# The first two modulation chunks in quarters, and the queries of layer 1 behind their keys

## The chip, the cores and the metric

The kernel runs on one core of a Trainium2 chip. The metric is device time of one launch in microseconds, the median of the runs. TensorE (PE) multiplies matrices, VectorE (DVE) and ScalarE (ACT) work on tiles elementwise, GpSimd (POOL) does a few elementwise jobs, and SyncE (SP) issues nearly all loads. Each engine works through its own list of instructions in order; semaphores tie the lists together.

## The reference

The program is a transformer of two layers on 256 tokens x and 256 context tokens, width 1024, all in float32. In a layer, nine modulation chunks of 1024 numbers are computed from the conditioning vectors and a weight `w_ada`. The first two of layer 0 are the shift and the scale of its first feed-forward block:

```python
silu_c = jax.nn.silu(c)
silu_cc = jax.nn.silu(c_ctx)
for l in range(DEPTH):
    mx = jnp.split((silu_c @ w_ada[l] + b_ada[l])[:, None, :], N_MOD, axis=-1)
    mc = jnp.split((silu_cc @ w_ada[l] + b_ada[l])[None, None, :], N_MOD, axis=-1)
    x = x + 0.5 * mx[2] * swiglu(modulate(rms_norm(x, norm_g[l, 0]), mx[0], mx[1]), w_ffn1_gu[l], w_ffn1_down[l])
    # the same for h_ctx with mc
    zx = modulate(rms_norm(x, norm_g[l, 1]), mx[3], mx[4]) @ w_in[l]
    zc = modulate(rms_norm(h_ctx, norm_g[l, 1]), mc[3], mc[4]) @ w_in[l]
    # split zx, zc: neighbourhood attention (qa, ka, va), window attention with rotary
    # positions (qb, kb, vb), convolution (u), three gates; merged, added to x; then a second ffn
```

`modulate(h, shift, scale)` is `h * (1 + scale) + shift`, and `swiglu` is `(silu(a) * b) @ w_down` with a and b the halves of `h @ w_gu`.

## The kernel before

**Tiles.** Activations lie with features on the 128 partitions: the residual is eight tiles `R[k]` of 128 x 512, x in the left half of the columns and context in the right. A weight block is 128 x 128. All float32 products are made of three faster ones: a number is split into a high part h (written by ACT, line 123) and the rest l (written by DVE, line 124), and `mm3` (lines 317 to 319) adds h·h, h·l and l·h. The weight stream `W` loads eight blocks at a time (`raw`, 512 KB, line 274, four buffers) and splits four at a time into `wh` and `wl`. A pool of 62 slots of 128 x 516 holds the other tiles.

**The start.** Class `FirstNorm` begins the first feed-forward block. With A = g(1 + scale) from chunk 1 and B = shift from chunk 0, the block's input is H = A·R·rs + B, where rs is one number per token from the sum of squares. To have work before rs is known, the first four output columns of the gate-and-up weight are multiplied with Q = A·R (`scale`, lines 511 and 512), and rs is applied to the result. These four results are the PSUM tiles `f` (12 `mm3` steps a feature tile, 96 matmuls for all eight). What B adds to them is a separate small product (`fb`, `fc`). Chunk 1 therefore stands ahead of all, and chunk 0 is needed only for H.

A chunk comes in two halves of four feature tiles. `ada_load` (line 190) loads a half as eight `araw` tiles of 256 KB. `ada_first` multiplies them with silu(c) (line 200; 32 output rows a matmul, four column groups), DVE copies the result (`adas`, 207), PE transposes it (`adat`, 209), and DVE adds the bias into `mod` (212) and, for chunk 1, makes `modA` (176, 178). `blocks` writes the whole start out in the order in which every engine is to do it, and `in_order` ties it so: half 0 of chunk 1, Q of tiles 0 to 3, all four columns on these, squares, half 1, Q of tiles 4 to 7, the columns on these, rs (`inv_rms`, lines 338 to 360), then `nt` = A·R·rs (459), chunk 0, `fb` (598), and Hh and Hl (484, 485). From `g` on, PE streams over the remaining 40 columns.

**Layer 1's attention.** `middle` runs over 12 attention steps: three head pairs of the neighbourhood attention, then three of the window attention, two query halves each. A step makes scores (`sc`, line 1008), a softmax (`pf`, 1041 to 1053), transposes (`pt`, 1069) and the product with the values (`pv`, 1088). Between these, PE is filled from a list of parts: gates, the window attention's keys (`key_b`), its queries (`query_b`), and merges. A key or query of the window attention passes through `rope`: ACT scales it (896), DVE makes four products with the sine (899), POOL multiplies and adds (901, 902), and ACT and DVE split it into `kbh` or `qx`. The order of the parts is a written list; `step` takes from it at an even rate, and more where a query is due.

Of the kernel before, what the change touches and what calls it, by code (L numbers as in the profile page):

```python
# [23 lines left out]
DFF = 2816  # L24
KF = 22
GRID_W = 64
# [35 lines left out]
WB, WS = 8, 4  # L62
# [25 lines left out]
def dit_block_kernel(ctx, tc, xT, vec, ident_d, const, crow, gfin, rpb, ws, ada0, adaT, out):  # L88
# [17 lines left out]
    def S(dt=F32, name="s"):  # L106
        return slots.tile([P, 2 * NQ], dt, tag="s", name=nm(name))
# [8 lines left out]
    def PS(name="ps"):  # L116
        return psum.tile([P, NT], F32, tag="ps", name=nm(name))
# [66 lines left out]
                out=modG[l][:, br], in0=src, scalar1=0.5, scalar2=None, op0=ALU.mult  # L184
            )

    def ada_load(ch, h):
        raws = [S(name="araw") for _ in range(KD)]
        for k in range(KD):
            nc.sync.dma_start(raws[k][:, :NT], ada0[ch, h, k])  # L190
        return raws

    def ada_first(ch, raws):

        for h in range(2):
            pa = PS("ada")
            for k in range(KD):
                raw = raws[h][k]
                for j in range(4):
                    nc.tensor.matmul(  # L200
                        pa[32 * j:32 * j + 32, :P], cs[:, k, :], raw[:, j * P:(j + 1) * P],
                        start=(k == 0), stop=(k == KD - 1),
                    )
                if k < KD - 1:
                    yield
            sa = S(name="adas")
            nc.vector.tensor_copy(sa[:, :P], pa[:, :P])
            pt = PS("adat")
            nc.tensor.transpose(pt[:, :P], sa[:, :P], ident)
            ks = slice(4 * h, 4 * h + 4)  # L210
            o = V_BADA + ch * KD
            nc.vector.tensor_tensor(
                out=mod[0][:, ch * KD + ks.start:ch * KD + ks.stop, :],
                in0=pt[:, :P].rearrange("p (j q) -> p j q", q=32)[:, :, 0:2],
                in1=vt[:, o + ks.start:o + ks.stop].unsqueeze(2).to_broadcast([P, 4, 2]), op=ALU.add,
            )
            mod_chunk(0, ch, ks)
            yield

    class Ada:  # L220

# [41 lines left out]
    class Stream:  # L263
# [38 lines left out]

        def col(self, name, l, c, n=KD):
            return [self.one(name, l, k * P, c) for k in range(n)]

        def wide(self, name, l, r, cs):
            o = (self.pos % WS) * P
# [195 lines left out]
    class FirstNorm(Norm):  # L503
# [19 lines left out]
            in_order(self.begin, self.end, N_AFTER)  # L523

        def blocks(self, fns):
            wts, pss, gens, res = [], [], [], []

            def block():
                wts.append(fns[len(wts)]())
                pss.append(PS("f"))  # L530
                gens.append(steps(pss[-1], wts[-1], self.Q, slice(0, NT)))

            def go(gen, n=1):
                for _ in range(n):
                    next(gen, None)

            def load_x(ks):
                for k in ks:
                    nc.sync.dma_start(R[k], xT[:, k, :])


            raws = [ada_load(1, 0)]
            W.load()
            load_x(range(4))
            W.load()
            load_x(range(4, KD))
            W.load()
            W.load()
            raws.append(ada_load(1, 1))
            chunk = ada_first(1, raws)  # L550
            go(chunk, KD)
            zero = [ada_load(0, 0), ada_load(0, 1)]
            W.load()
            zero = ada_first(0, zero)
            self.scale(0)
            block()
            go(gens[0])
            for k in range(1, 4):
                self.scale(k)
                go(gens[0])  # L560
            block()
            go(gens[1], 4)
            for k in range(4):
                self.square(k, nc.vector)
            block()
            go(gens[2], 4)
            for k in range(4, KD):
                self.square(k, nc.vector)
            block()
            go(gens[3], 4)  # L570
            norm = inv_rms([self.sq], self.nq, oneD, res)
            go(chunk, KD)
            for k in range(4, KD):
                self.scale(k)
                go(gens[0])
            go(norm)
            go(gens[1], 4)
            go(norm)
            self.rs = res[0]
            go(gens[2], 4)  # L580
            nts = [self.normed(k) for k in range(KD - N_POOL)]
            go(zero, KD)
            go(gens[3], 4)


            b = mod[0][:, :KD, :]
            bb = cpool.tile([P, KD, 4], F32R, name="bb")
            n = len(wts)
            self.H, brs = [], []
            for h in range(2):  # L590
                ks = slice(4 * h, 4 * h + 4)
                split(bb[:, ks, 0:2], bb[:, ks, 2:4], b[:, ks])
                self.hidden(range(4 * h, min(4 * h + 4, KD - N_POOL)), nts)
                pb = PS("fb")
                for i, w in enumerate(wts):
                    for k in range(ks.start, ks.stop):
                        for j in range(2):
                            nc.tensor.matmul(
                                pb[:4, i * P:(i + 1) * P], bb[:, k, :], w[k][j],
                                start=k == ks.start and j == 0, stop=k == ks.stop - 1 and j == 1)  # L600
                br = S(name="br")
                nc.vector.tensor_copy(br[:4, :n * P], pb[:4, :n * P])
                brs.append(br)
                if h == 0:
                    go(zero, KD)
            for _ in range(N_EARLY):
                W.make()
            self.end = traced()
# [34 lines left out]
    def ffn(l, br, norm, nxt, ada_end=None):  # L643
# [7 lines left out]
        pend = norm.first([lambda c=c: W.col(name + "_gu", l, c) for c in cols[:nf]], 3)  # L651
        if ada_end:
            ada.enter(mod[l][:, 3 * br * KD, 0:1])
        n0 = ada.n
# [43 lines left out]
    def middle(l, norm, nxt):  # L698
# [563 lines left out]
def pack(inputs, plan):  # L1262
# [33 lines left out]
            blk = a[name][l, r:r + P, c:c + P]  # L1296
        ws[i // WB, :, i % WB] = blk

    ada0 = np.ascontiguousarray(a["w_ada"][0][:, :2 * D].reshape(KD, P, 2, 2, NT).transpose(2, 3, 0, 1, 4))
# [8 lines left out]

SHAPES = {
    "xT": (P, KD, NT), "vec": (P, V_N), "ident_d": (P, P), "const": (P, C_N), "crow": (2, D), "gfin": (1, D),  # L1310
    "rpb": (DEPTH, 6, P, 6 * GRID_W), "ws": (N_WT // WB, P, WB * P), "ada0": (2, 2, KD, P, NT), "adaT": (N_ADA, P, D),
}


# [16 lines left out]
```

## Time and profile before

| | |
|---|---|
| median of 3 runs | 1968.12 us (1966.95 to 1969.37) |
| profiled execution | 1965.63 us, span 1963.8 us |
| PE busy | 1938.2 us (99%) |
| DVE, ACT, POOL busy | 71%, 46%, 5% |
| PE's longest idle times after the first 60 us | 2.80 us and 1.51 us, both in layer 1's attention |
| granted clock, mean | 0.997 |

A row of the timeline gives start and duration in us, engine, line, operation, tiles out<-in, shapes and count; in brackets stands the idle time of the engine ahead of it and what ended that. Rows of the same kind that follow each other are merged, so the duration of a row with x8 covers eight instructions. A row of the windows gives, for each engine, busy us and instructions in a stretch, then the clock granted to PE, the DMA engines' busy share and the rate in GB/s. The profiled execution was 2.5 us below the median of the runs.

### The profile page before, as it was taken

Reading aid. Unit: us, or ns where it says so; the run is one execution under the profiler, and the core shown is the slowest. Engines: PE = TensorE matmul, PEld = TensorE weight load, DVE = VectorE, ACT = ScalarE, POOL = GpSimd, SP = SyncE. Lnnn points to the kernel's source line nnn. Section 1 sums busy time; section 2 is a strip of 40 time slices with the busy share of each in tenths; the row PEclk is TensorE's granted clock in tenths of the full one; section 3 lists DMA queues with packets and bytes.
Section 4 is the critical chain, followed back from the end, with each engine's and each line's share of the span. In section 5 each row is a group of like instructions: output and inputs, shape, how many; then the busy total and the mean of one; then the engine's idle time right before and its main releaser. Section 6 shows DMA issues by size and latency. Waiting matters only on the chain. (4 is left out here: it accounts for less than half of the span.)

```text
span 1963.8 us, 29316 instructions
## 1 busy us (share of the span) xinstructions
PE 1938.2 (99%) x10748; PEld 1649.4 (84%) x10748; DVE 1401.6 (71%) x3190; ACT 896.9 (46%) x1765; POOL 104.4 (5%) x100
## 2 busy tenths in 40 slices
PE   7999999999999999999999999999999999999998
PEld 4788888897888888988888888888888988999998
DVE  5897667779777546976667569666675897887654
ACT  3533232353767634533323344332223567866553
POOL 0000000100011101000000110000001001120000
PEclk9999999999999999999999999999999999999999
DMA  8365454522221222354444435544544243355553
GB/s 306 129 237 171 161 182 161 183 89 95 85 71 65 97 95 89 120 180 150 160 162 161 159 110 174 168 144 159 164 157 142 95 146 117 129 183 182 184 185 106
DMA packets 82655, 287.39 MB, mean 146 GB/s; under 512 B 9296, under 2 KB 11088, under 8 KB 82128
## 3 DMA queue, kind: packets, MB, share of 16 engines
q1 hardware_dynamic: 79488, 277.91, 42.9%
q0 software_dynamic: 864, 4.98, 0.7%
q10 hardware_dynamic: 2160, 2.64, 0.5%
q8 instruction: 84, 1.38, 0.3%
q14 instruction: 59, 0.48, 0.1%
HBM read 284.44 MB, written 1.05 MB: 145 GB/s over the span
## 5 line engine op out<-in xcount | busy, mean ns | idle before, releaser
L123 ACT ACTIVATE wh<-raw 128x512 fp32r<-128x512 f32 x760 | 463.9, 627 | 541.0 <-PE g L318 163.4
L124 DVE TENSOR_TENSOR wl<-raw,wh 128x512 fp32r<-128x512 f32 x760 | 520.4, 695 | 161.6 <-ACT wh L123 156.5
L244 DVE CUSTOM_DVE_ANT_0 junk<-araw,phase 128x512 f32<-128x512 f32 x512 | 353.3, 690 | 231.0 <-DMA araw<-in_adaT_dram 220.8
L319 PE MATMUL g<-Hh,wl 128*128 128x512 f32 (+1 forms) x1240 | 455.2, 367 | 0.0
L318 PE MATMUL g<-Hl,wh 128*128 128x512 f32 (+1 forms) x1240 | 454.4, 366 | 0.0
L317 PE MATMUL g<-Hh,wh 128*128 128x512 f32 (+1 forms) x1240 | 454.3, 366 | 0.0
L317 PEld LDWEIGHTS g<-Hh,wh 128*128 128x128 f32 x1240 | 233.3, 188 | 41.4 <-ACT wh L123 0.3
L318 PEld LDWEIGHTS g<-Hl,wh 128*128 128x128 f32 x1240 | 233.0, 188 | 41.4
L319 PEld LDWEIGHTS g<-Hh,wl 128*128 128x128 f32 x1240 | 232.9, 188 | 40.8
L317 PE MATMUL pr<-gh,wh 128*128 128x512 f32 (+1 forms) x704 | 257.7, 366 | 0.0
L319 PE MATMUL pr<-gh,wl 128*128 128x512 f32 (+1 forms) x704 | 257.5, 366 | 0.0
L318 PE MATMUL pr<-gl,wh 128*128 128x512 f32 (+1 forms) x704 | 257.0, 365 | 0.0
L317 PE MATMUL b<-Hh,wh 128*128 128x512 f32 (+1 forms) x480 | 166.1, 346 | 0.0
L318 PE MATMUL b<-Hl,wh 128*128 128x512 f32 (+1 forms) x480 | 163.1, 340 | 0.0
L319 PE MATMUL b<-Hh,wl 128*128 128x512 f32 (+1 forms) x480 | 163.0, 340 | 0.0
L123 ACT ACTIVATE gh<-g 128x512 fp32r<-128x512 f32 (+1 forms) x88 | 50.7, 576 | 234.2 <-DVE g L685 226.6
L318 PEld LDWEIGHTS pr<-gl,wh 128*128 128x128 f32 x704 | 132.4, 188 | 23.2
L319 PEld LDWEIGHTS pr<-gh,wl 128*128 128x128 f32 x704 | 132.4, 188 | 23.0
L317 PEld LDWEIGHTS pr<-gh,wh 128*128 128x128 f32 x704 | 132.2, 188 | 22.9
L317 PE MATMUL f<-qh,wh 128*128 128x258 f32 (+1 forms) x408 | 123.0, 302 | 4.0 <-ACT wh L123 2.4
L319 PE MATMUL f<-qh,wl 128*128 128x258 f32 (+1 forms) x408 | 120.2, 295 | 1.1 <-DVE wl L124 1.1
L318 PE MATMUL f<-ql,wh 128*128 128x258 f32 (+1 forms) x408 | 120.5, 295 | 0.0
(246 smaller groups left out, 2590.1 us busy)
## 6 DMA issues: line engine op xcount, KB each, us to landing
raw<-in_ws_dram SPq DMA_DIRECT2D x380, 512.0 KB, 3.6
araw<-in_adaT_dram SPq DMA_DIRECT2D x128, 512.0 KB, 4.2
araw<-in_ada_dram SPq DMA_DIRECT2D x32, 256.0 KB, 5.4
phase<-in_crow_dram POOLq DMA_DIRECT2D x3, 1024.0 KB, 5.8
tb<-in_rpb_dram ACTq DMA_DIRECT2D x12, 192.0 KB, 2.6
R<-in_xT_dram SPq DMA_DIRECT2D x8, 256.0 KB, 6.3
phase<-in_const_dram POOLq DMA_DIRECT2D x2, 640.0 KB, 6.6
out_dram<-fin SPq DMA_DIRECT2D x4, 256.0 KB, 2.5
```

What stands on the lines that cost most here:

```text
L123: nc.scalar.activation(out=hi, in_=src, func=AF.Copy)
L124: nc.vector.tensor_tensor(out=lo, in0=src, in1=f32(hi), op=ALU.subtract)
L244: nc.vector.tensor_tensor_reduce(out=junk, in0=raw[:, c], in1=self.rows[:, s, c], scale=1.0, scalar=0.0, op0=ALU.mult, op1=ALU.add, accum_ ...
L317: nc.tensor.matmul(ps, wh, xh, start=start, stop=False)
L318: nc.tensor.matmul(ps, wh, xl, start=False, stop=False)
L319: nc.tensor.matmul(ps, wl, xh, start=False, stop=stop)
```

## The change

It has two parts.

**The start.** A chunk is loaded and computed by quarters of two feature tiles. A quarter has four `araw` tiles of 256 KB (the bytes of a chunk stay the same); each holds rows of two feature blocks, so that the sums over the even and the odd ones land in different column groups, and the transpose becomes a product with `sel`, a 128 x 4 matrix that adds the two. The 16 rows of weights that the four columns need are taken by feature tile, not by column: the list `ws` is packed in the order of use, so one `wh` now holds one feature tile of all four columns. Loads are queued quarter by quarter: four `araw`, one `raw`, two `R`; chunk 0 comes behind all of them. The work goes by feature tile: weights, Q, the four columns' products, and so on, with the next quarter's chain between.

```diff
+    sel = cpool.tile([P, 4], F32, name="sel")
     def ada_first(ch, q, raws):
+        for i, raw in enumerate(raws):
+            for h in range(2):
+                for j in range(2):
+                    o = 2 * h + j
                     nc.tensor.matmul(
+                        pa[32 * o:32 * o + 32, :P], cs[:, 2 * i + h, :], raw[:, o * P:(o + 1) * P],
+                        start=(i == 0), stop=(i == len(raws) - 1),
+        nc.vector.tensor_copy(sa[:, :P], pa[:, :P])
+        yield
+        nc.tensor.matmul(pt[:, :4], sa[:, :P], sel, start=True, stop=True)
 ...
+            a = ada_first(1, 0, raws[0])
+            go(a)
+            go(a)
+            for q in range(4):
+                k = 2 * q
+                if q < 2:
+                    raws.append(ada_load(1, q + 2))
+                    W.load()
+                    load_x(k + 4, k + 5)
+                weights(k)
+                self.scale(k)
+                prod(k)
+                if q < 3:
+                    a = ada_first(1, q + 1, raws[q + 1])
+                    go(a)
+                weights(k + 1)
+                self.scale(k + 1)
+                if q == 3:
+                    break
+                prod(k + 1, range(2))
+                go(a)
+                prod(k + 1, range(2, n))
+                self.square(k, nc.vector)
+                self.square(k + 1, nc.vector)
+            zero = [ada_load(0, q) for q in range(4)]
+            W.load()
+            W.load()
+            self.square(KD - 2, nc.vector)
+            self.square(KD - 1, nc.vector)
             norm = inv_rms([self.sq], self.nq, oneD, res)
+            prod(KD - 1, [0, 1])
+            z = [ada_first(0, q, raws) for q, raws in enumerate(zero)]
 ...
```

Behind this stand chunk 0's four quarters with the rest of tile 7's products, rs, `fb`, `nt` and H between them.

On DVE, the order before, from the end of a half's chain (`mod`, `modA`): the Q of four tiles and the weights of two columns follow at once.

```order
L212 TENSOR_TENSOR mod_103<-adat_192,vt 128x8
L176 TENSOR_SCALAR modt_195<-mod_103 128x8
L178 TENSOR_TENSOR modA_104<-modt_195,vt 128x8
L512 SCALAR_TENSOR_TENSOR ql_233<-R_79,modA_104,qh_232 128x256 x2
L124 TENSOR_TENSOR wl_239<-raw_125,wh_238 128x512
L124 TENSOR_TENSOR wl_243<-raw_125,wh_242 128x512
L512 SCALAR_TENSOR_TENSOR ql_251<-R_80,modA_104,qh_250 128x256 x2
L512 SCALAR_TENSOR_TENSOR ql_260<-R_81,modA_104,qh_259 128x256 x2
L512 SCALAR_TENSOR_TENSOR ql_269<-R_82,modA_104,qh_268 128x256 x2
```

Now, from the end of one quarter's chain to the end of the next:

```order
L178 TENSOR_TENSOR modA_104<-modt_322,vt 128x4
L396 TENSOR_TENSOR sq_245<-sq_245,sq_331 128x512
L396 TENSOR_TENSOR sq_245<-sq_245,sq_334 128x512
L124 TENSOR_TENSOR wl_338<-raw_172,wh_337 128x512
L522 SCALAR_TENSOR_TENSOR ql_342<-R_83,modA_104,qh_341 128x256 x2
L213 COPY adas_376<-ada_359 128x128
L124 TENSOR_TENSOR wl_379<-raw_172,wh_378 128x512
L522 SCALAR_TENSOR_TENSOR ql_383<-R_84,modA_104,qh_382 128x256 x2
L219 TENSOR_TENSOR mod_103<-adat_394,vt 128x4
L176 TENSOR_SCALAR modt_397<-mod_103 128x4
L178 TENSOR_TENSOR modA_104<-modt_397,vt 128x4
```

The squares' additions moved ahead of the next tile's weights and Q, and the copy of a quarter's result (`adas`) stands behind the first tile's Q.

On PE, at the same place, before: the two halves of a column's work enclose one chain.

```order
L319 MATMUL f_350<-qh_268,wl_343 128x512
L200 MATMUL ada_363<-araw_141,cs_100 32x128 x4
L200 MATMUL ada_363<-araw_142,cs_100 32x128 x4
L200 MATMUL ada_363<-araw_143,cs_100 32x128 x4
L200 MATMUL ada_363<-araw_144,cs_100 32x128 x4
L200 MATMUL ada_363<-araw_145,cs_100 32x128 x4
L200 MATMUL ada_363<-araw_146,cs_100 32x128 x4
L200 MATMUL ada_363<-araw_147,cs_100 32x128 x4
L200 MATMUL ada_363<-araw_148,cs_100 32x128 x4
L209 MATMUL adat_398<-ident,adas_396 128x128
L317 MATMUL f_246<-qh_404,wh_242 128x512
```

Now (the last of a tile's twelve products, the next quarter's chain, and half of the next tile's products ahead of `adat`):

```order
L329 MATMUL f_114<-qh_341,wl_338 128x512
L208 MATMUL ada_359<-araw_250,cs_100 32x128 x4
L208 MATMUL ada_359<-araw_251,cs_100 32x128 x4
L208 MATMUL ada_359<-araw_252,cs_100 32x128 x4
L208 MATMUL ada_359<-araw_253,cs_100 32x128 x4
L327 MATMUL f_111<-qh_382,wh_378 128x512
L328 MATMUL f_111<-ql_383,wh_378 128x512
L329 MATMUL f_111<-qh_382,wl_379 128x512
L327 MATMUL f_112<-qh_382,wh_378 128x512
L328 MATMUL f_112<-ql_383,wh_378 128x512
L329 MATMUL f_112<-qh_382,wl_379 128x512
L216 MATMUL adat_394<-sel,adas_376 128x4
```

The chain is entered four times instead of two, each time behind twelve products, and its second half behind six more.

**Layer 1's list of parts.** The number of parts is the same; the window attention's keys and first query come after six gates, the other queries after two more.

```diff
-            parts = [query(2), *some(0, 8), *some(2, 1), key_b(), query_b(0), *some(2, 3), query_b(1),
-                     *some(2, 4), query_b(2), *some(1, 4)]
+            parts = [query(2), *some(0, 6), key_b(), query_b(0), *some(0, 2), query_b(1), query_b(2),
+                     *some(2, 8), *some(1, 4)]
```

On ACT, before, ahead of the first scores of the window attention (`qx_14828` is their query; the keys were split a step earlier):

```order
L1053 ACTIVATE pf_13979<-pf_13979,st_14795 128x512
L1053 ACTIVATE pf_13980<-pf_13980,st_14801 128x512
L896 ACTIVATE rot_13992<-qb_14738 128x256
L934 ACTIVATE gate_14687<-b_14831,hb_13994 128x256
L123 ACTIVATE wh_14967<-raw_14965 128x512
L123 ACTIVATE wh_15003<-raw_14965 128x512
L123 ACTIVATE wh_15009<-raw_15007 128x512
L123 ACTIVATE qx_14828<-rot_13992 128x256
L123 ACTIVATE wh_15048<-raw_15007 128x512
L934 ACTIVATE gate_14958<-b_14870,hb_13994 128x256
L123 ACTIVATE pt_13981<-pt_14910 128x512
```

Now the same place holds the second and the third query; the first (`qx_14647`) was split two steps earlier:

```order
L1095 ACTIVATE pf_14011<-pf_14011,st_14835 128x512
L1095 ACTIVATE pf_14012<-pf_14012,st_14841 128x512
L938 ACTIVATE rot_14024<-qb_14778 128x256
L123 ACTIVATE wh_15016<-raw_15014 128x512
L123 ACTIVATE wh_15052<-raw_15014 128x512
L123 ACTIVATE wh_15058<-raw_15056 128x512
L123 ACTIVATE qx_14868<-rot_14024 128x256
L938 ACTIVATE rot_14024<-qb_14871 128x256
L123 ACTIVATE pt_14013<-pt_14959 128x512
L123 ACTIVATE pt_14015<-pt_14966 128x512
L123 ACTIVATE pt_14017<-pt_14973 128x512
L123 ACTIVATE pt_14019<-pt_14980 128x512
```

The query that the next scores need has left this place, and two other queries stand there, ahead of the transposes' splits.

Apart from the start and layer 1's attention, the instructions of every engine stand in the same order as before.

More of the change, by code (lines that the diff above doesn't have):

```diff
@@ L185, in mod_chunk @@
             )
[L187 to L190, printed above, removed]
-        return raws
[L193 to L199, printed above, removed]
+    sel = cpool.tile([P, 4], F32, name="sel")
+    nc.vector.tensor_tensor(
+        out=sel.rearrange("p (j s) -> p j s", j=2),
+        in0=ident[:, :64].rearrange("p (j q) -> p j q", j=2)[:, :, 0:2],
+        in1=ident[:, 64:].rearrange("p (j q) -> p j q", j=2)[:, :, 0:2], op=ALU.add)
@@ L200, in ada_first, with ada_load @@
+    def ada_load(ch, q):
+        raws = [S(name="araw") for _ in range(KD // 2)]
+        for i, raw in enumerate(raws):
+            nc.sync.dma_start(raw[:, :NT], ada0[ch, q, i])
+        return raws
+    def ada_first(ch, q, raws):
+        pa = PS("ada")
+        for i, raw in enumerate(raws):
+            for h in range(2):
+                for j in range(2):
+                    o = 2 * h + j
                     nc.tensor.matmul(
-                        pa[32 * j:32 * j + 32, :P], cs[:, k, :], raw[:, j * P:(j + 1) * P],
@@ L202, in ada_first @@
-                        start=(k == 0), stop=(k == KD - 1),
-                    )
[L204 to L216, printed above, removed]
@@ L220, in dit_block_kernel @@
+        nc.vector.tensor_tensor(
+            out=mod[0][:, ch * KD + ks.start:ch * KD + ks.stop, :],
+            in0=pt[:, :4].rearrange("p (j s) -> p j s", j=2),
+            in1=vt[:, o + ks.start:o + ks.stop].unsqueeze(2).to_broadcast([P, 2, 2]), op=ALU.add,
+        )
+        mod_chunk(0, ch, ks)
     class Ada:
@@ L304, in col, with rows @@
             return [self.one(name, l, k * P, c) for k in range(n)]
+        def rows(self, name, l, c, n=KD):
+            for k in range(n):
+                yield self.one(name, l, k * P, c)
         def wide(self, name, l, r, cs):
@@ L525, in blocks @@
         def blocks(self, fns):
[L526 to L537, printed above, removed]
+            n = len(fns)
+            gens = [f() for f in fns]
+            wts, pss, res = [[] for _ in fns], [PS("f") for _ in fns], []
@@ L538, in load_x, with go, weights, prod @@
+            def load_x(*ks):
                 for k in ks:
                     nc.sync.dma_start(R[k], xT[:, k, :])
[L542 to L546, printed above, removed]
+            def go(gen):
+                next(gen, None)
+            def weights(k):
+                for w, g in zip(wts, gens):
+                    w.append(next(g))
+            def prod(k, which=range(n)):
+                for i in which:
+                    mm3(pss[i], wts[i][k], [t[:, :NT] for t in self.Q[k]], k == 0, k == KD - 1)
@@ new lines, in blocks @@
+            raws = []
+            for q in range(2):
+                raws.append(ada_load(1, q))
+                W.load()
+                load_x(2 * q, 2 * q + 1)
+            a = ada_first(1, 0, raws[0])
[22 more added lines that the diff above has]
+                self.square(k + 1, nc.vector)
@@ L547, in blocks @@
+            zero = [ada_load(0, q) for q in range(4)]
             W.load()
             W.load()
[L549 to L561, printed above, removed]
@@ L589, in blocks, with parts_of, product_of @@
-            self.H, brs = [], []
-            for h in range(2):
+            pbs, brs = [], []
+            def parts_of(h):
                 ks = slice(4 * h, 4 * h + 4)
                 split(bb[:, ks, 0:2], bb[:, ks, 2:4], b[:, ks])
-                self.hidden(range(4 * h, min(4 * h + 4, KD - N_POOL)), nts)
+            def product_of(h):
                 pb = PS("fb")
                 for i, w in enumerate(wts):
-                    for k in range(ks.start, ks.stop):
+                    for k in range(4 * h, 4 * h + 4):
@@ L650, in ffn @@
         todo = cols[nf:]
-        pend = norm.first([lambda c=c: W.col(name + "_gu", l, c) for c in cols[:nf]], 3)
+        if isinstance(norm, FirstNorm):
+            pend = norm.first([lambda c=c: W.rows(name + "_gu", l, c) for c in cols[:nf]], nf)
+        else:
+            pend = norm.first([lambda c=c: W.col(name + "_gu", l, c) for c in cols[:nf]], 3)
         if ada_end:
```

66 lines of the change are left out of this document (37 added, 29 removed).

## Prediction

> **What bounds the kernel now.** I read the page first, then PE's waits, then the timeline of the first 62 us and of the attention of layer 1.
>
> ```profile
> PE 1938.2 (99%) x10748; PEld 1649.4 (84%) x10748; DVE 1401.6 (71%) x3190; ACT 896.9 (46%) x1765; POOL 104.4 (5%) x100
> PE sc L1008 <- ACT qx L123: 4.3, 2, 2.8
> PE ada L200 <- ACT cs L152: 4.0, 1, 4.0
> PE adat L209 <- DVE adas L207: 3.5, 4, 2.2
> PE f L317 <- ACT wh L123: 2.4, 1, 2.4
> PE f L317 <- ACT qh L511: 1.6, 1, 1.6
> ```
>
> The first row is the page's busy time; the others are PE's waits (total, times, longest, in us). PE bounds the kernel: beside the start and two places in the attention it waits for almost nothing. Whatever makes PE's stream begin later or stop is paid in full, and whatever shortens these waits is gained in full. So the forecast is two differences: when the stream of `g` begins, and what is left of the 4.3 us.
>
> The start is not held by one resource alone:
>
> ```profile
> 15.00:20.00 5.00, 4.99 (x19) 3.89 (x19) 4.66 (x10) 5.00 (x11) 0.00 (x0) 1.00 1.04 413
> 25.00:30.00 5.00, 4.46 (x74) 3.48 (x74) 1.02 (x3) 0.00 (x0) 0.00 (x0) 1.00 1.05 387
> 30.00:35.00 5.00, 3.26 (x9) 2.17 (x10) 3.92 (x12) 3.90 (x9) 0.00 (x0) 0.84 1.06 393
> 35.00:40.00 5.00, 5.00 (x23) 4.17 (x23) 1.05 (x5) 0.96 (x2) 0.00 (x0) 0.81 1.03 407
> 45.00:50.00 5.00, 2.76 (x55) 2.27 (x44) 4.07 (x13) 0.96 (x4) 0.00 (x0) 1.00 0.00 0
> ```
>
> Busy us per engine (PE, PEld, DVE, ACT, POOL), then PE's clock, DMA share and GB/s. The loads run at their limit early and are over by 45 us; from then on DVE leads. In 60 us PE idles in a few blocks only, since each chain of a chunk lies between 27 to 48 products that need nothing from it.
>
> ```profile
> 6.37 0.20 PEld L200 LDWEIGHTS ada<-araw,cs 128*32 128x32 f32 x8 [0.47 <-DMA araw<-in_ada_dram]
> 13.71 0.63 PE L318 MATMUL f<-ql,wh 128*128 128x512 f32 x1
> 14.14 0.63 PE L319 MATMUL f<-qh,wl 128*128 128x512 f32 x1
> 17.01 0.39 PE L317 MATMUL f<-qh,wh 128*128 128x512 f32 x1
> 17.24 0.39 PE L318 MATMUL f<-ql,wh 128*128 128x512 f32 x1
> 20.31 1.29 DVE L124 TENSOR_TENSOR wl<-raw,wh 128x512 fp32r<-128x512 f32 x2
> 21.51 3.08 DVE L386 TENSOR_TENSOR sq<-sq,sq 128x512 f32<-128x512 f32 x4
> 27.75 1.96 PE L200 MATMUL ada<-araw,cs 128*32 128x128 f32 x64
> 29.77 0.29 DVE L207 COPY adas<-ada 128x128 f32<-128x128 f32 x1 [3.98 <-PE ada L200]
> 30.11 0.33 PE L209 MATMUL adat<-ident,adas 128*128 128x128 f32 x1 [0.41 <-DVE adas L207]
> 30.48 0.17 DVE L212 TENSOR_TENSOR mod<-adat,vt 128x8 f32<-128x8 f32 x1 [0.42 <-PE adat L209]
> 30.68 0.17 DVE L176 TENSOR_SCALAR modt<-mod 128x8 f32<-128x8 f32 x1
> 30.88 0.17 DVE L178 TENSOR_TENSOR modA<-modt,vt 128x8 f32<-128x8 f32 x1
> 31.63 3.37 DVE L512 SCALAR_TENSOR_TENSOR ql<-R,modA,qh 128x256 fp32r<-128x256 f32 x8 [0.58 <-ACT qh L511]
> 32.05 0.49 PE L317 MATMUL f<-qh,wh 128*128 128x512 f32 x1 [1.60 <-ACT qh L511]
> ```
>
> These rows of the timeline are the prices. Matmuls of 512 columns start 0.23 us apart at full clock (17.01, 17.24) and 0.43 apart before it (13.71, 14.14). Half a `wl` row is 0.65, a quarter of the `sq` row 0.77, a tile's `ql` (two of eight) 0.84. A quarter of a chunk has half of the 64 `ada` records: 0.98. From one engine's end to the next one's start pass 0.04 to 0.05 us (29.77 + 0.29 to 30.11).
>
> **The change, the start.** The work is the same: 96 `f` matmuls, 256 `ada` records, as many loads, as many splits. What is new is the order, and it makes a loop. DVE adds two squares, makes `wl` and `ql` of tile k, and then stands at `adas`, which needs the next quarter's `ada` on PE, behind twelve products of tile k, behind that `ql`. Behind the waiting `adas` stand `wl` and `ql` of tile k+1, whose inputs are there; PE waits for these after its first product, and `adat` stands behind five more. Only then come `mod` and `modA`, for which the next Q waits. One turn:
>
> - DVE: 2 x 0.77 + 0.65 + 0.84 = 3.03
> - PE: eleven matmuls from the first `L318` on, 2.53, and `ada` 0.98 with 0.1 until its last result is out: 3.6
> - DVE: `adas` 0.29, `wl` 0.65, `ql` 0.84: 1.78
> - PE: five matmuls 1.16 and `adat` 0.33: 1.5
> - DVE: three small ones at 0.2: 0.6; five handovers 0.25
>
> That is 10.7 us for a quarter, against 5.2 us that its 2 MB take at some 400 GB/s and 6.8 us of PE's own work (24 x 0.23 + 0.98 + 0.3). The loads are hidden by the loop from the second quarter on; chunk 0, now at the end of SP's queue, has landed near 36 us (48 pieces of 256 KB ahead of and in it, 0.65 us each at 400 GB/s, from 4 us on) and is wanted at 47. ACT's `qh` and `wh` lie under DVE's three microseconds.
>
> `adat` as a product with four columns has no row; the nearest are 0.33 (same weights, 128 columns) and the `fc` row below, 0.12 each. I take 0.33, the row with the same weights to load; all eight together are worth (0.33 - 0.12) x 8 = 1.7 us at most. `sel` costs DVE one small operation while it waits for the first chunk.
>
> First quarter: its fourth `araw` lands at 6.37, and 0.24 + 0.1 + 0.29 + 0.33 + 0.6 and handovers put `modA` at 8.4, where it stood at 11.3. Second: no squares (9.2), and some eight matmuls and part of `ada` at the lower clock, 1.4 more: 19.0. Third, with one addition: 28.9. Fourth: 39.6. In the kernel before the last of `modA` was there at 31.05. Then 3.03 for tile 6, 17 matmuls (3.9) to 46.6, `ada` and `sums` 1.5, and the root, `diag` and `rstd` with two more chains between, 4.4 us: rs at 52.5.
>
> ```profile
> 41.61 0.60 ACT L360 ACTIVATE rs<-rstd 128x512 f32<-128x512 f32 x1 [3.47 <-PE rstd L358]
> 42.24 5.97 DVE L459 SCALAR_TENSOR_TENSOR nt<-R,modA,rs 128x256 f32<-128x256 f32 x12 [2.98 <-ACT rs L360]
> 49.68 3.29 DVE L485 SCALAR_TENSOR_TENSOR Hl<-nt,mod,Hh 128x256 fp32r<-128x256 f32 x8 [0.23 <-ACT Hh L484]
> 59.03 0.68 DVE L602 COPY br<-fb 4x512 f32<-4x512 f32 x1 [0.35 <-PE fb L598]
> 60.44 1.72 PE L613 MATMUL fc<-pick,br 4*128 4x2 f32 x14
> 62.09 0.50 PE L317 MATMUL g<-Hh,wh 128*128 128x512 f32 x1
> ```
>
> Before, rs was there at 42.2. Behind it DVE sets the pace in both: `nt` 5.97, twelve `Hl` 4.94, two `br` 1.36, copies and small ones 1.2, the first `wl` 0.65 make 14.1, and the waits for `ada` and for ACT between them 1.7. This gives 68.3 for the third `g` product, so a stream from 67.8. Before, the stream is unbroken from 62.09 with four `g` products done, as if from 61.2. The difference is 6.7 us. The same sum made for the program before ends its second `br` at 59.0 instead of 59.71, so I add 0.7.
>
> The clock is left. After the 1.60 us in which PE idled ahead of 32.05, the windows show 0.84 and 0.81: together (0.16 + 0.19) x 5 x 2, some 3.5 us at half clock. The new loop has two waits of 1.7 to 2.0 us per turn (3.03 less what overlaps, and 1.78), so I put in one such stretch; eight matmuls fill it at 0.43 instead of 0.23: 1.5. The start costs 8.9 us, with ends of 6.7 (no such stretch, no 0.7) and 11.9 (three).
>
> By the Trainium skill (TensorE: Matmul & The Clock Gate, Part 1) the clock is halved only after an idle window of about 3.4 us; no wait in the loop is that long, so by the page the stretch would not be there and the start would cost 7.4. The row of 30 to 35 us disagrees, with 3.26 us of PE work in 5.
>
> **The change, layer 1.**
>
> ```profile
> 1647.37 1.72 DVE L899 SCALAR_TENSOR_TENSOR rot<-qb,phase 32x256 f32<-32x256 f32 x4 [1.33 <-ACT rot L896]
> 1649.23 1.16 POOL L902 TENSOR_TENSOR rot<-rot,rot 128x256 f32<-128x256 f32 x1 [1.07 <-DVE rot L899]
> 1650.42 0.42 ACT L123 ACTIVATE qx<-rot 128x256 fp32r<-128x256 f32 x1 [1.17 <-POOL rot L902]
> 1650.89 0.50 PE L1008 MATMUL sc<-kbh,qx 64*128 64x512 f32 x2 [2.80 <-ACT qx L123]
> 1652.11 3.24 PE L1069 MATMUL pt<-ident,pf 128*128 128x128 f32 x16
> 1672.48 1.97 PE L1069 MATMUL pt<-ident,pf 128*128 128x128 f32 x16
> 1692.99 0.50 PE L1008 MATMUL sc<-kbh,qx 64*128 64x512 f32 x2 [1.51 <-ACT qx L123]
> 1648.00:1656.00 8.00, 5.20 (x30) 4.48 (x30) 7.13 (x14) 4.80 (x11) 1.32 (x2) 0.79 0.23 74
> ```
>
> The first window query goes through ACT, DVE, POOL and ACT while PE stands 2.80 us; then the clock is halved, and the sixteen transposes take 3.24 instead of 1.97 and the scores 0.3 more. The third query costs 1.51 later. In the new list the first query is split two steps earlier, some 12 us before its scores, and the third five steps before its own. Both waits go, with the half clock: 2.80 + 1.51 + 1.27 + 0.3 = 5.9 us. More cannot be gained here. What is late next: the second and third query stand on DVE (1.72 each) and ACT ahead of the transposes' splits, for which `pv` waits; 57 fill matmuls at 0.12 and the transposes cover them by about 0.4 us. If that cover is gone by the length of one rope (1.7 + 1.2), 3.0 of the 5.9 is left; I take 5.9, since the query's path is known and the cover is positive.
>
> **Sum.** 8.9 - 5.9 = 3.0 us more. The profiled execution was 1965.6, and would be 1968.6; the runs' median lies 2.5 above it, so 1971.1.
>
> **Rivals.** About 0.2%, 3.9 us, is what a measurement of this kernel can tell from no change.
>
> *Loads set the pace (faster).* If DVE did not hold the loop, PE's 6.8 us would: the fourth `modA` at 8.4 + 3 x 6.8 = 28.8 instead of 39.6, the total 1960. For it: the loads are at their limit until 40 us, and the first `modA` comes 2.9 us earlier. Against: DVE's order leaves no way round `adas`. It decides if the fourth `modA` is there by 33. Chance 0.08.
>
> *The clock is halved again and again (slower).* Each of the loop's long waits can fall into one window; two or three more stretches at 1.5 give 1975. For it: the two places quoted. Against: PE's 2.2 us wait for `adas` lies in the window of 45 to 50, which has 2.76 us of PE work in 5 and clock 1.00. From one more stretch on it is slower than before. Chance 0.20.
>
> *The clock stays full.* 1.5 us less: 1969.6. Chance 0.12. By the rule of the Trainium skill above, this is the case to expect.
>
> *The attention gets a new wait.* `pv` waits behind the second rope: 3.0 gained instead of 5.9, so 1974. Chance 0.15.
>
> **Numbers.** The forecast has 0.40, with its own range of 1968.5 to 1973; 0.05 is for what I don't see, on either side. The range of 1966 to 1976 leaves out most of the first rival and the worst of the second. Slower by over 0.2% means over 1972.1: 0.12 of the forecast, all of the second rival, most of the last, in all 0.43; faster 0.10; the rest, 0.47, is within it.
>
> **What would show it.** Right: the four `modA` near 8, 19, 29 and 40 us; `adas` on DVE waiting for PE once a turn; `L318` waiting for `ql` 1.7 to 2.0 us twice a turn; rs near 53 and an unbroken `g` near 69; no wait for `qx` at `L1008`, clock 1.00 there. Wrong: turns of 5 to 7 us, or `L1008` or `pv` waiting anew.

## The result, and the profile after

The changed kernel takes 1980.22 us (median of six runs, 1976.35 to 1982.47); the kernel before, run beside it, 1967.96 us (1966.76 to 1969.37). The ratio is 1.006 with a 95% interval of 1.0047 to 1.0073: 9 to 14 us slower. The forecast was 1971.1, 3.0 us above the kernel before, with a range of 1966 to 1976. The kernel did get slower, by some four times as much, and the range lies below the result.

The profiled execution after (1982.47 us) lies 2.2 above its kernel's median, that of before 2.3 below its own. The two traces therefore stand some 17 us apart, where the medians stand 12.3 apart; sizes below are taken from the medians, places from the traces. Of the 16.9 us between the two spans, 15.5 are there at the first scores of layer 1's attention (1607.2 us after, 1591.7 before). So nearly the whole lag is made ahead of the attention (some 11 us of it, if the two executions are set back to their medians), and the new list, which was to win 5.9 us in the attention, wins nothing.

PE's waits after, in the form of those quoted of before (total, times, longest, in us):

```profile
PE f L328 <- DVE ql L522: 7.4, 6, 1.4
PE fb L615 <- DVE bb L124: 4.0, 1, 4.0
PE b L327 <- DVE rot L941: 3.2, 1, 3.2
PE g L327 <- ACT Hh L123: 1.8, 1, 1.8
PE f L327 <- ACT qh L521: 1.6, 1, 1.6
PE ada L208 <- DMA araw<-in_ada_dram: 1.4, 3, 0.8
```

The first row is the loop of the new start: two waits for `ql` in each of three turns. The two waits for `qx` (4.3 us) are gone. Three rows are there that the forecast does not have: `fb` for `bb` (0.8 us before), `g` for a high part of H, and a gate's product `b` for a rope's DVE work.

The four `modA` of the timeline, the ends of the four quarters' chains of chunk 1, and rs:

```profile
9.45 0.16 DVE L178 TENSOR_TENSOR modA<-modt,vt 128x4 f32<-128x4 f32 x1
21.01 0.17 DVE L178 TENSOR_TENSOR modA<-modt,vt 128x4 f32<-128x4 f32 x1
30.84 0.17 DVE L178 TENSOR_TENSOR modA<-modt,vt 128x4 f32<-128x4 f32 x1
41.48 0.16 DVE L178 TENSOR_TENSOR modA<-modt,vt 128x4 f32<-128x4 f32 x1
53.96 0.60 ACT L370 ACTIVATE rs<-rstd 128x512 f32<-128x512 f32 x1 [0.56 <-PE rstd L368]
```

The windows of the start (busy us of PE, PEld, DVE, ACT, POOL; then PE's clock, DMA share, GB/s):

```profile
25.00:35.00 10.00, 7.17 (x57) 4.89 (x56) 4.87 (x12) 3.79 (x8) 0.00 (x0) 1.00 1.05 392
35.00:45.00 10.00, 7.17 (x57) 4.88 (x56) 5.43 (x14) 3.30 (x8) 0.00 (x0) 1.00 0.48 179
60.00:65.00 5.00, 1.41 (x14) 1.44 (x15) 4.49 (x14) 1.80 (x5) 0.00 (x0) 0.55 0.00 0
65.00:70.00 5.00, 4.66 (x39) 4.22 (x36) 4.74 (x12) 4.22 (x10) 0.00 (x0) 0.76 0.01 2
70.00:75.00 5.00, 5.00 (x16) 3.88 (x15) 3.81 (x9) 2.65 (x6) 3.84 (x2) 0.66 0.62 226
```

Between 25 and 45 us PE stands for almost three us in ten, and DVE is busy only half of the time: neither engine bounds the start, the chain between them does. The clock is full there (1.00, and products of 512 columns start 0.23 us apart). It is low from 60 us on, behind the loop.

### The profile page after: what moved, and what is told of

Read it like the earlier page. It is cut to its first block, busy times and chain, and to the rows that moved or that the text cites. A ratio compares the mean times of both kernels' runs of the same rounds, so it can differ in the third digit from the quotient of the medians.

```text
span 1980.7 us, 29367 instructions
## 1 busy us (share of the span) xinstructions
PE 1947.2 (98%) x10760; PEld 1655.7 (84%) x10760; DVE 1400.4 (71%) x3203; ACT 898.3 (45%) x1765; POOL 106.2 (5%) x100
## 4 chain that ended last, share of the span: by engine, by line
PE 94%; DVE 2%; issue 1%; ACT 1%; DMA 1%; POOL 0%; SPq 0%; ACTq 0%; DVEq 0%; POOLq 0%
PE g L329 13%; PE g L328 13%; PE g L327 13%; PE pr L328 8%; PE pr L327 8%; PE pr L329 8%; PE b L327 4%; PE b L328 4%; PE b L329 4%; PE f L328 3%; PE f L329 3%; PE f L327 3%; PE sc L1050 1%; PE pv L1130 1%; PE pt L1111 1%
```

## The experiments

The theory after the result: in layer 1 the gain of 5.9 us never came, because the third query holds a bank of PSUM, where PE's products land; and the start costs 11.5 to 14 us, by the loop and by the waits and the clock behind it. The rivals: the start costs the 8.9 us forecast, and the list gives its 5.9 us after all or costs 3.4; or the two parts disturb each other. A time below is the median of 5 or 11 executions, with those of the kernel before beside them.

### Each part alone

The new list in the kernel before, nothing else:

```diff
-            parts = [query(2), *some(0, 8), *some(2, 1), key_b(), query_b(0), *some(2, 3), query_b(1),
-                     *some(2, 4), query_b(2), *some(1, 4)]
+            parts = [query(2), *some(0, 6), key_b(), query_b(0), *some(0, 2), query_b(1), query_b(2),
+                     *some(2, 8), *some(1, 4)]
```

> The kernel before with the new list of parts for layer 1 and nothing else. Theory (from the trace after): the waits for qx at the first and third window query go (4.3 us), but a gate's product stands some 3.3 us for the bank of PSUM that the third query holds until its rope is through DVE, and the clock is halved around it; net between 0 and +1.5 us against before. Rival (the forecast): the waits go, nothing comes for them, -5.9 us. Second rival: the start costs only the 8.9 us forecast and the list the rest of the 12.3 us, +3.4 us.

The changed kernel with the list of before (the diff the other way round):

> The kernel with the new start and the old list for layer 1. Theory: PE's stream of g comes 13.8 us later and the total is 11.5 to 14 us above before; the half clock behind the wait for bb and at tile 7's H is there as in the kernel with both parts. Rival (the forecast of the start): +8.9 us. The two waits for qx at the scores are 2.8 and 1.5 us as before.

The list alone: ratio 0.9998 (0.9989 to 1.0006), 1967.22 against 1967.46 us. The start alone: 1.0044 (1.003 to 1.0057), 1976.27 us, some 8.6 us more. So neither of the rivals on the list holds: it brings nothing and costs nothing. And the start's cost is at the forecast's 8.9, below the 11.5 to 14 that I had now expected from one trace: here the theory misses and the forecast is right.

What became of the list's 5.9 us stands in the trace of the list alone. The scores of the first window query no longer wait, and 7 us later a gate's product does:

```profile
1649.61 0.50 PE L1008 MATMUL sc<-kbh,qx 64*128 64x512 f32 x2
1652.69 0.42 ACT L123 ACTIVATE qx<-rot 128x256 fp32r<-128x256 f32 x1 [1.58 <-POOL rot L902]
1653.60 0.38 ACT L896 ACTIVATE rot<-qb 128x256 f32<-128x256 f32 x1 [0.49 <-DVE qx L124]
1654.45 1.77 DVE L899 SCALAR_TENSOR_TENSOR rot<-qb,phase 32x256 f32<-32x256 f32 x4
1656.37 0.55 PE L317 MATMUL b<-Hh,wh 128*128 128x256 f32 x1 [3.21 <-DVE rot L899]
```

Read upwards from the last row. The gate's product waits for DVE's `rot` of the third query: not for its numbers, which no gate uses, but for the bank of PSUM that the query's `qb` occupies until ACT and DVE have read it. The kernel's pool has eight banks (line 98), used in turn; between this `qb` and the product stand one gate, two score tiles and four tiles of transposes, so the product is the eighth after it. The third query's rope cannot begin before 1653.60: on ACT its first step stands behind the `qx` of the second query, which waits for POOL. It also writes over the same tile, since all ropes share one pair of `rot` tiles (`N_ROT`, line 78); the row at 1653.60 shows ACT waiting for DVE's `qx`, the last to read it. The wait of the product is 3.21 us, where the two that went were 2.80 and 1.51.

The clock goes with it. The windows of the list alone, and the same windows before:

```profile
1652.00:1656.00 4.00, 1.16 (x11) 0.96 (x9) 3.84 (x9) 2.82 (x7) 1.38 (x2) 1.00 0.40 121
1656.00:1660.00 4.00, 3.63 (x18) 3.66 (x19) 3.93 (x11) 2.71 (x7) 0.74 (x1) 0.57 0.04 14
```

```profile
1648.00:1652.00 4.00, 1.20 (x7) 0.58 (x6) 3.84 (x7) 2.55 (x6) 1.32 (x2) 0.92 0.11 22
1652.00:1656.00 4.00, 4.00 (x25) 3.90 (x24) 3.29 (x7) 2.25 (x5) 0.00 (x0) 0.65 0.35 126
```

In both kernels a window with 1.2 us of PE work in four is followed by one at about 0.6 of the clock. Only the place has changed: in the kernel before it hit the transposes, with the new list the gates.

### The queries apart

If it is the two queries in a row, a gate between them must take the wait away (the new list, and this one):

```diff
-            parts = [query(2), *some(0, 6), key_b(), query_b(0), *some(0, 2), query_b(1), query_b(2),
-                     *some(2, 8), *some(1, 4)]
+            parts = [query(2), *some(0, 6), key_b(), query_b(0), *some(0, 2), query_b(1), *some(2, 1), query_b(2),
+                     *some(2, 7), *some(1, 4)]
```

> The kernel before with the new list for layer 1 but one gate between the second and the third window query. Theory (the new wait comes of two queries in a row, whose ropes follow each other through ACT and whose bank is wanted eight allocations later): the gate's wait of 3.2 us falls below 1 us, the waits for qx stay away, 2 to 6 us below before. Rival (any early third query holds a bank): a wait of over 2 us remains and the time is that of before.

Measured with the start of before: 0.9986 (0.9977 to 0.9995), 1964.58 against 1967.95 us, about 2.7 us faster (3.4 in the medians). The gate's product at the old place, from the timeline, and the longest of PE's waits in layer 1's attention of this kernel:

```profile
1655.20 0.39 PE L317 MATMUL b<-Hh,wh 128*128 128x256 f32 x1 [0.34 <-ACT gate L934]
PE mo L317 <- ACT y L123: 1.3, 1, 1.3
```

The wait of a gate for `rot` is gone; the product stands 0.34 us, for another gate's read. The theory holds: the bank is the cause of the wait, and the third query may come early if it does not follow the second at once. The windows show it too:

```profile
1652.00:1656.00 4.00, 3.65 (x32) 3.27 (x29) 3.91 (x9) 2.46 (x6) 1.26 (x2) 1.00 0.10 20
1656.00:1660.00 4.00, 4.00 (x36) 4.00 (x35) 4.00 (x12) 4.00 (x13) 0.84 (x1) 1.00 0.34 126
```

So even a clean list brings only about half of the 5.9 us. Against the trace of before, PE's work is 4.0 us later at the first scores of the attention and 1.4 us earlier at the third window query's, so 5.4 us are won on the way. Of these 1.9 are lost at the end: there the merges wait 1.27 us for the last `y` (row `mo`, above), which the kernel before does not, and a group of products that takes 2.12 us there takes 4.00. Part of what PE gains it waits out where it next meets ACT; 3.4 us are left in this trace.

A second list was tried that keeps the order of before and moves keys, first query and third query up by one gate each, so that the queries stay three gates or more apart:

```diff
-            parts = [query(2), *some(0, 8), *some(2, 1), key_b(), query_b(0), *some(2, 3), query_b(1),
-                     *some(2, 4), query_b(2), *some(1, 4)]
+            parts = [query(2), *some(0, 8), key_b(), query_b(0), *some(2, 4), query_b(1),
+                     *some(2, 3), query_b(2), *some(2, 1), *some(1, 4)]
```

> The kernel before with a list in which the keys and the first window query stand one gate earlier, the third query one gate earlier, and the queries stay apart by three gates or more. Theory (bank of PSUM held by two queries in a row): no wait for qx, no wait of a gate for DVE's rot, clock 1.00 in the attention, -4 to -6 us against before. Rival (moving a query earlier always puts its rope in the way of something): a new wait of 2 to 3 us, and between -2 and +1 us.

It gives 0.9989 (0.998 to 0.9998), 1.4 us in the medians: no wait for `qx`, none for `rot`, clock 1.00 in the attention, and the same 1.27 us at the end. The waits came out as the theory has them. The size did not: it lies in the range of the rival (-2 to +1), and the rival's new wait is there too, though of 1.27 us in place of 2 to 3 and at the end of the attention.

### The loop of the start

Is it the loop that holds the start, or is it the loads? The same work in another order (list of before; the diff against the changed kernel, `...` for lines left out):

```diff
+            weights(0)
             for q in range(4):
 ...
-                weights(k)
                 self.scale(k)
-                prod(k)
-                if q < 3:
-                    a = ada_first(1, q + 1, raws[q + 1])
-                    go(a)
                 weights(k + 1)
                 self.scale(k + 1)
+                prod(k)
                 if q == 3:
                     break
-                prod(k + 1, range(2))
-                go(a)
-                prod(k + 1, range(2, n))
                 self.square(k, nc.vector)
                 self.square(k + 1, nc.vector)
+                a = ada_first(1, q + 1, raws[q + 1])
+                go(a)
+                weights(k + 2)
+                prod(k + 1, [0])
+                go(a)
+                prod(k + 1, range(1, n))
```

> The new start (old list for layer 1) with the turn's order changed: both tiles' Q and the second tile's weights stand ahead of the copy of the next quarter's result on DVE, the squares fill the wait, adat stands behind three products. Loads, banks and amount of work as in the new start. Theory (the loop DVE-PE-DVE-PE-DVE sets the 10.7 us a turn): turns of 6.8 to 7.5 us, rs near 44, 8 to 11.5 us below the kernel with the new start alone. Rival (loads at their limit, or the clock, set the pace): turns stay above 9.5 us, less than 4 us gained.

1968.59 us, ratio 1.0004 (0.9995 to 1.0013); beside it the new start took 1976.27. Some 7.7 us are gone by order alone, just short of the 8 to 11.5 expected. The four `modA` of this kernel, two of its windows, and DVE's rows for `adas` in the first 60 us of the changed kernel and the first 45 us of this one (busy, mean ns, idle ahead of it):

```profile
L178 DVE TENSOR_TENSOR modA<-modt,vt x4: 161/161/163, 8.9 to 32.0; 128x4 f32<-128x4 f32 x4
20.00:30.00 10.00, 10.00 (x90) 7.68 (x92) 7.51 (x17) 5.80 (x13) 0.00 (x0) 1.00 1.05 399
30.00:40.00 10.00, 10.00 (x94) 7.96 (x86) 5.34 (x13) 4.60 (x9) 0.00 (x0) 1.00 1.03 393
```

```profile
L213 DVE COPY adas<-ada 128x128 f32<-128x128 f32 x8 | 2.3, 290 | 20.9 <-PE ada L208 20.9
```

```profile
L213 DVE COPY adas<-ada 128x128 f32<-128x128 f32 x7 | 2.0, 290 | 11.2 <-PE ada L208 11.2
```

From the first `modA` to the last a turn takes 7.7 us in place of 10.7, a little over the 6.8 to 7.5 expected. The standing at `adas` is almost halved, and PE does not stop between 10.1 and 48 us. While the loads run they have the same rate in both kernels (392 GB/s in the window of 25 to 35 us above, 399 and 393 here), so they do not set the pace of the new start. The loop is shown.

### The wait for `bb` and the clock behind the loop

Two kernels take the 4.0 us wait of `fb` away in opposite ways, both with the new start and the list of before. One fills it:

```diff
             parts_of(1)
+            dummy = PS("dummy")
+            for i in range(16):
+                nc.tensor.matmul(dummy, wts[i % n][KD - 1][0], self.Q[KD - 1][0][:, :NT], start=i == 0, stop=i == 15)
             product_of(1)
```

> The kernel with the new start alone, and 16 products of 512 columns into a bank that nobody reads, put on PE ahead of the second half of the small product of chunk 0, where PE stands 4.0 us for bb. It adds work to the reference's computation, and leaves none out. Theory (the idle PE brings the clock to half for 7 to 14 us behind it, which costs 2 to 5 us): clock 1.00 from 15 to 80 us, 2 to 5 us below the kernel with the new start. Rival (DVE's nt and H set the time of the first g products, the half clock lies under them): within 1 us of it.

The other moves `bb` ahead on DVE:

```diff
+            go(z[3])
+            parts_of(1)
             rows_of(0)
             nts += [self.normed(k) for k in (2, 3)]
             self.hidden(range(2), nts)
-            go(z[3])
-            parts_of(1)
             product_of(1)
```

> The kernel with the new start alone, with the last quarter of chunk 0 and the second half of bb ahead of two nt and two H on DVE. Theory (the wait for bb is only DVE's order; DVE's sum of nt, H and br sets the first g): the wait of 4.0 us falls below 1, PE waits for H or br instead about as long, total within 1.5 us of the kernel with the new start, less by up to 3 us if the clock then stays full. Rival (the wait for bb is itself on the path): 3 to 4 us below it.

And the new start itself, for comparison:

> The kernel with the new start alone once more, beside the two that change one thing in it. Its first profile was of a slow execution: 13.8 us later at the stream of g. Theory: the median lies 8 to 12 us above before, and the executions differ by the number of stretches at half clock behind the wait for bb.

The three ratios are 1.0052 (1.0039 to 1.0066), 1.0053 (1.004 to 1.0065) and 1.0043 (1.003 to 1.0056). In the medians the two stand 2.0 and 1.8 us above the new start itself, within what its own executions scatter by (1974.8 to 1983.1 in these and the first five): nothing is gained, and no difference is clear of the noise. With the wait filled, PE's next wait is the first row; with `bb` ahead, the second:

```profile
PE fc L655 <- DVE br L622: 1.6, 1, 1.6
```

```profile
PE fc L652 <- DVE br L622: 5.0, 1, 5.0
PE fb L615 <- DVE bb L124: 0.8, 1, 0.8
```

What PE no longer waits for at `fb` it waits for at `fc`, where DVE's copy `br` comes late. This agrees with the forecast, in which DVE's sum of `nt`, H and `br` behind rs sets the first `g`; the 4.0 us are no cost of their own. The price of the clock could not be set apart. The windows of the kernel with the wait filled, and of the new start itself:

```profile
60.00:65.00 5.00, 4.55 (x24) 3.51 (x25) 4.49 (x13) 0.89 (x3) 0.00 (x0) 1.00 0.00 0
70.00:75.00 5.00, 5.00 (x17) 4.31 (x17) 4.61 (x8) 3.32 (x8) 2.01 (x2) 0.50 0.41 123
```

```profile
60.00:65.00 5.00, 1.14 (x12) 1.17 (x13) 4.50 (x14) 1.70 (x5) 0.00 (x0) 0.79 0.00 0
70.00:75.00 5.00, 5.00 (x16) 4.22 (x16) 4.55 (x7) 2.73 (x6) 2.01 (x2) 0.50 0.50 157
```

With PE kept busy the clock is full at first (1.00 in place of 0.79), and halved later all the same (0.50 in both), behind the wait at `fc`. The gains of 2 to 5 us by a full clock and of 3 to 4 us by an earlier `bb` did not come. The other side of each pair, no change within 1 and 1.5 us, is nearer, though both medians lie a little above it.

### Do the parts add up?

The kernel with both parts once more:

> The kernel with both parts once more. Theory (the parts add up: 8.6 us for the start by two runs, -0.3 for the list): 6 to 11 us above before. Rival (the parts disturb each other): 12 us or more above it, as in its first runs.

1.0058 (1.0045 to 1.007), 11.3 us in the medians, between the two numbers expected. Since the start alone had given 1.0044 and 1.0043, all three were then timed beside one another:

> Both parts, beside each part alone on one chip. Theory (the parts add up): this run minus before equals the sum of the next two within 2.5 us. Rival (they disturb each other): 4 us or more above that sum.

> The new start alone: 7 to 11 us above before, by the two earlier runs of it 8.6.

> The new list alone: between -1 and +3 us against before; the earlier run gave -0.3. If the parts add up to the 11 to 12 us of both, it lies at the upper end or the start does.

| | both parts | start alone | list alone |
|---|---|---|---|
| first time | 1.0060 (1.0047 to 1.0073) | 1.0044 (1.0030 to 1.0057) | 0.9998 (0.9989 to 1.0006) |
| again | 1.0058 (1.0045 to 1.0070) | 1.0043 (1.0030 to 1.0056) | |
| side by side | 1.0049 (1.0035 to 1.0062) | 1.0057 (1.0044 to 1.0069) | 1.0000 (0.9991 to 1.0008) |

Side by side the start alone gives 11.2 us, a little over the 7 to 11 expected, the list alone nothing, and both give 9.6: the parts do not disturb each other. The start alone moved by 3 us from one timing to the next, and its single executions by 8. The means of the three columns are 11.0, 9.4 and -0.2 us; the 1.6 us between the first two are within this scatter.

### A version that beats both

Behind the broken loop, what is left is DVE's tail. Here the squares are all summed by the third turn, rs is made ahead of the last twenty products, and chunk 0's chains and `nt` run between these; the list is the second one above, with the queries three gates or more apart. Some of the new lines, `...` for those left out:

```diff
+                for j in ((0, 1), (2, 3, 4), (5, 6, 7))[q]:
+                    self.square(j, nc.vector)
 ...
+            norm = inv_rms([self.sq], self.nq, oneD, res)
 ...
+            prod(KD - 2, [0])
+            go(norm)
+            prod(KD - 2, range(1, n))
 ...
+            go(z[0])
+            prod(KD - 1, [0])
+            go(z[0])
+            nts += [self.normed(k) for k in (0, 1)]
```

> The loop of the run with the chain early, and behind it rs, nt and chunk 0's chains drawn in among the last twenty products, the parts of bb ahead of nt and H, and the list of parts with the queries apart. Theory (after the loop is broken, what is left of the start is the 4.0 us wait for bb with its half clock and DVE's tail of nt and H behind rs, all of which PE's own products can cover): PE without a gap over 1 us between 10 and 80 us, 6 to 10 us below the kernel before. Rival (PE's own work and DVE's total bound the start, the tail only shifts): between -3 and +1 us against before.

0.9987 (0.9978 to 0.9995): 2.6 us faster, far less than the 6 to 10 expected and within the rival's -3 to +1. One row of PE's waits points at the reason, and it is of my own making: `br` stood behind all H on DVE, while `fc` stands ahead of the first `g` on PE:

```profile
PE fc L652 <- DVE br L585: 3.3, 1, 3.3
```

With the copies ahead of the later H, and chunk 0's last two chains drawn together, so that products cover them (the diff against the version just shown):

```diff
             go(z[2])
-            prod(KD - 1, [2])
-            go(z[2])
-            nts += [self.normed(k) for k in range(4, KD - N_POOL)]
             go(z[3])
+            nts += [self.normed(4)]
+            go(z[2])
             product_of(0)
-            self.hidden(range(2), nts)
             go(z[3])
             parts_of(1)
-            prod(KD - 1, [3])
+            nts += [self.normed(5)]
+            prod(KD - 1, [2])
             product_of(1)
+            prod(KD - 1, [3])
+            self.hidden(range(2), nts)
+            rows_of(0)
             W.make()
+            rows_of(1)
             self.hidden(range(2, 4), nts)
             W.make()
             self.hidden(range(4, KD - N_POOL), nts)
-            rows_of(0)
-            rows_of(1)
```

> As the run with rs early, but the copies of the small product (br) stand ahead of four H on DVE, so that fc no longer waits for them, and chunk 0's last chains are covered by the second half of the products of tile 7. Theory (the 3.3 us wait for br and the 10 us at half clock behind it are what that run lost): no gap over 1.2 us between 10 and 80 us, the stream of g from 53 us on, 7 to 11 us below before. Rival (DVE's nt and H bound the first g): a gap of the same length within g, less than 2 us gained on that run.

> The version with the loop broken, rs early, the copies ahead of H and the queries apart, once more: 5 to 9 us below before.

0.9962 (0.9949 to 0.9974) and 0.9958 (0.9945 to 0.997): 1961.06 and 1959.53 us, 7 to 8 us faster than the kernel before, in the first timing at the lower edge of the 7 to 11 expected, in the second within its 5 to 9. The windows of the start in the first:

```profile
20.00:30.00 10.00, 10.00 (x99) 7.63 (x98) 8.26 (x18) 6.06 (x13) 0.00 (x0) 1.00 1.04 398
30.00:40.00 10.00, 10.00 (x89) 7.63 (x91) 5.28 (x18) 4.38 (x8) 1.28 (x1) 1.00 1.03 396
40.00:50.00 10.00, 9.19 (x165) 7.81 (x158) 7.39 (x24) 2.91 (x9) 0.00 (x0) 1.00 0.05 17
50.00:60.00 10.00, 9.55 (x41) 7.43 (x41) 9.99 (x22) 8.08 (x18) 3.89 (x2) 0.83 0.37 139
```

From 10.1 us on PE stands for 0.6 us at most in one place, and DVE is full in the last ten us. The quarters themselves are no loss, then; the order in which they were entered was. Whether halves of a chunk, with rs drawn ahead in the same way, would do as well was not tried.

## Why the prediction was wrong

**The start** was forecast at 8.9 us (6.7 to 11.9) and measures 9.4 in the mean of three. The steps:

- The loop. Turns of 10.6, 9.9 and 10.7 us were forecast; `modA` shows 11.6, 9.8 and 10.6. The waits for `ql` are 1.4 us at most, not 1.7 to 2.0. Right, and the run with the turn's order changed shows that the loop is the cause. The first turn is longer because all twelve products of its first tile start 0.43 us apart, where eight had been put in.
- The first quarter ends 1.2 us later than the 8.4 forecast, since its `araw` tiles landed later (the last row of PE's waits above: 1.4 us in three places); rs is there 2.1 us later (54.56 against 52.5). In the other traces of the same start the first product of `f` comes from 1.0 us earlier to 1.3 us later than in this one.
- The clock. One stretch at half clock inside the loop was put in, for its two waits a turn. There is none in the loop from its second turn on (1.00 from 25 to 45 us) but several behind it: after the wait for `bb`, in the first products of `g`, and after the 1.8 us wait of `g` for H. The step was wrong in place and count. What it cost could not be set apart from DVE's tail.
- The tail. That DVE sets the pace behind rs fits the runs: taking the wait for `bb` away in two ways gained nothing. `g` begins at 69.6 us, near the 69 forecast, but is not unbroken: PE stands once more, 1.8 us up to 84.0.

**Layer 1** is where the forecast failed. The step was that both waits go, with the half clock, for 2.80 + 1.51 + 1.27 + 0.3 = 5.9 us, with 3.0 of it left if the cover over the second rope is gone. Measured: a gain of 0.2 us in the mean of two. Three things in it:

- The waits for `qx` did go, as forecast.
- I asked what is late next, and looked for it among those who wait for a result: `pv`, for the transposes' splits behind the second rope. The one that came waits for a place: the gate's product needs the bank that the third query's `qb` holds. The rows of ACT ahead of the prediction show that rope's first step behind the second query's `qx`; the bank behind it was not counted. Its price is 3.2 us and a half clock, where 2.9 was the most put down for the other wait.
- The 5.9 were an upper end, not the value. With the bank's wait taken away, 2.7 and 1.4 us come out in two lists: 1.9 us of what PE gains it loses again at the merges.

With 0 in place of the 5.9 the sum would have been 1977.0, within 3.2 us of the result. These 3.2 us are not accounted for; by the ratios the same kernel lay 11.8, 11.4 and 9.6 us above the kernel before in three timings, and part of them is that scatter. The rivals: "the attention gets a new wait" came true in kind, at another place and at twice its price; "the clock is halved again and again" in the number of stretches, not in their place. They had 1974 and 1975, because each was priced alone; both at once lie above the range. "The loads set the pace" is refuted by the loop's run.

Of the clock, the runs show four cases. In the loop, where PE's waits are 1.4 us at most, the clock stayed full, and behind the 4.0 us wait for `bb` it was low. In layer 1 it fell behind a wait of 3.21 us (0.57 in the window), and with the wait for `bb` filled it fell behind one of 1.60 us at `fc` (0.50). The rule of the Trainium skill (TensorE: Matmul & The Clock Gate, Part 1) by which the clock is halved after an idle window of about 3.4 us agrees with the first two. The third lies a little under it and the fourth far under it, and there the measurement decides.

## What to carry to other kernels

When work is moved earlier, ask not only who waits for its result but who waits for the buffer that it holds until its last reader is through; two of a kind in a row hold two, and the second reader queues behind the first on every engine in between. Ask the same of scratch tiles that the two share. Taking a wait of PE away is a gain only if the engines that it meets next are early enough as well: take the wait's length as the upper end of the gain, and look at the next place where PE meets them. And where a chain runs back and forth between two engines of which neither is full, order is worth trying before work is cut: here another order of the same rows moved the time by 8 us, and one more behind it, together with the second list, by nearly as much again.

## What the runs showed of the hardware

The clock fell not only behind idle stretches. In the best version PE stands nowhere for over 0.6 us between 10.1 and 80 us, and yet the window of 50 to 60 us has the clock at 0.83; between 37.5 and 53.6 us lie some 10 us of narrow products (`ada` with 32 rows of result, 4.1 us; `fb` and `fc` with 4 rows or columns, 4.2 and 2.1). In the loop of the new start, ten-us windows with 7.17 us of mostly wide products (512 columns) kept 1.00. That narrow products count for less in whatever grants the clock would fit both. It was not tested by itself, so it stays a guess.
